# First norm summed on VectorE, columns of both streams at once, background sums put off, unread products on TensorE

## The chip, the cores and the metric

The kernel runs on one core of one Trainium2 chip. A core has five engines with queues of their own: TensorE (PE in the profile; its weight loads are shown as PEld), VectorE (DVE), ScalarE (ACT), GpSimd (POOL) and SyncE (SP), and 16 DMA engines that move data between the chip's memory and the core's own. An engine takes its instructions in order. The metric is the device time of one execution in microseconds (us); the time of a kernel is the median of its runs.

## The reference

Two layers over a stream of 256 latent tokens and a stream of 256 context tokens, with 1024 features. Each layer is an FFN, a token mixer (latent attention in layer 0, windowed attention in layer 1) and an FFN. What matters here is the first sub-layer of layer 0:

```python
cond_x = jax.nn.silu(c)
cond_c = jax.nn.silu(c_ctx)
mx = jnp.split((cond_x @ mod_w[layer] + mod_b[layer])[:, None, :], N_MOD, axis=-1)
mc = jnp.split(cond_c @ mod_w[layer] + mod_b[layer], N_MOD, axis=-1)
x = x + 0.5 * mx[2] * swiglu(modulate(rms_norm(x, norm_g[layer, 0]), mx[0], mx[1]), ffn_w_in[layer, 0], ffn_w_out[layer, 0])
xc = xc + 0.5 * mc[2] * swiglu(modulate(rms_norm(xc, norm_g[layer, 0]), mc[0], mc[1]), ffn_w_in[layer, 0], ffn_w_out[layer, 0])
...
rms_norm(x, g) = x * rsqrt(mean(x * x, axis=-1) + 1e-6) * g
modulate(h, shift, scale) = h * (1.0 + scale) + shift
swiglu(h, w_in, w_out): g, u = split(h @ w_in, 2); (silu(g) * u) @ w_out
```

Shift, scale and gate of all nine chunks come from one product of the conditioning vectors with mod_w (the adaLN). It is needed before the first normalised input exists: chunks 0 and 1 first, chunk 2 when the first FFN adds its result, the others later.

## The kernel before

The activations lie transposed: 8 tiles of 128 features (k = 0 to 7) by 512 columns, 256 latent tokens and 256 context tokens. Each float32 operand of a large product is split in a high half (rounded by ACT, L182) and a low half (the rest, by VectorE or POOL, L183), and `mm3` issues three matmuls for a pair: high by high (L210), high by low (L211), low by high (L212). Weights come as 128x1024 tiles through a ring of three raw buffers, four high and four low ones. One output tile of the FFN's first product is 8 k by 3 = 24 matmuls of 512 columns.

The order within each engine's queue is set by a scheduler when the kernel is built; `behind` holds an instruction back until another has been issued. SP issues nearly all DMAs, in order.

The start runs as follows. SP loads the constants (`load_const`, L66), the 8 tiles of x (L76), then for each k the four parts of the adaLN columns of chunks 0 and 1 (`load_column`, L120, tensor `modo`), with four first weights (`win`) between them. The norm: ACT squares each x tile (L823), TensorE sums over features by a product with ones into one bank of 128x512 (L824), so every partition holds the sum of every token; ACT takes the root (L841) and VectorE the reciprocal (L842) over 128x256 for each stream, into the strips `rstds`. For each k `mod_on_pe` multiplies the conditioning vectors by the columns (L128), ACT copies the result (L131), TensorE transposes it (L133), and VectorE adds the two halves and the bias and forms 1 + scale times the norm's gain, for one stream after the other (L138 to L140). `inputs(k)` then scales x for each stream (VectorE, L847) and makes the high (ACT, L849) and low half (VectorE, L850) of the first FFN's input.

As soon as input k exists, it is multiplied by the weights of the first four output tiles that are there by then, the lead weights (`lead_products`, `lead_weight`). Their low halves are made on POOL (L183, `wlo<-big,whi`), one at the start, the others after k = 1, 3 and 5.

Then `ffn` runs over 22 tiles f in three groups (8, 7, 7), with two weights each: gate (`og`) and up (`ou`). Between tiles `pump` issues steps of the background work: `mod_in_background` sums the adaLN of chunks 2 to 7 on VectorE, one k tile of mod_w per step, with one 128x1024 sum per stream (L149, L151), and after eight of these two small steps. Chunk 2 is needed when group 0 closes. `closing` has a step for each of the outputs d.

## Time and profile before

| | |
|---|---|
| median of 3 runs | 1734.75 us (1734.36 to 1736.54) |
| profiled execution | 1734.44 us |
| its span, first to last instruction | 1732.5 us |
| TensorE busy | 1682.6 us, 97% |
| VectorE busy | 1065.3 us, 61% |
| ScalarE busy | 666.9 us, 38% |
| GpSimd busy | 185.2 us, 11% |
| mean granted TensorE clock | 0.991 |
| HBM read and written | 240.11 and 1.05 MB |

A row of the timeline gives start and duration in us, the engine, the line of the kernel, the operation, output<-inputs with shapes and types, how many instructions the row merges (x), and in brackets how long the engine had been idle before and what ended that. "SPq" is a DMA issue of SP. A row of a waits view gives the waiting engine and line, the one waited for, the total in us, how often, and the longest. A row of the groups gives line, engine, operation, count | busy time and mean ns of one | idle time before. Granted clock 1.00 is full speed. Chains and waits are inferred, and a busy TensorE is not TensorE at its peak.

### The profile page before, as it was taken

The numbers are of one execution on the slowest core, as the hardware profiler recorded it, in microseconds if no ns is written. First come the engines' busy times: TensorE is split into PE (matmuls) and PEld (weight loads), VectorE is DVE, ScalarE is ACT, GpSimd is POOL, SyncE is SP. The second block draws the span as 40 slices with busy tenths as digits, with TensorE's granted clock in tenths as the row PEclk, the third lists the DMA queues.
The fourth block names the chain that finished last, engine by engine and source line by source line (L and its number), as shares of the span: only waits on it lengthen the run. The fifth ranks groups of instructions, "written<-read, shape, count | busy, mean of one in ns | idle before, by whom it ended". The sixth has DMA issues, their size and how long they took to land.

```text
span 1732.5 us, 24034 instructions
## 1 busy us (share of the span) xinstructions
PE 1682.6 (97%) x9512; PEld 1440.9 (83%) x9512; DVE 1065.3 (61%) x1592; ACT 666.9 (38%) x1135; POOL 185.2 (11%) x183
## 2 busy tenths in 40 slices
PE   7999999999999999999999999999999988989997
PEld 4688888888788898888888898888888888889997
DVE  4877576645667567856946374635433589755554
ACT  4322222225556352222222352222222577554443
POOL 1000000004132130000000220000000452110001
PEclk9999999999999999999999999999999999999998
DMA  8566355431212136644645254634222221145553
GB/s 331 187 199 195 129 188 189 147 125 64 86 49 72 51 98 203 198 147 156 219 126 172 93 173 160 215 121 161 94 98 92 93 85 46 53 148 182 173 191 99
DMA packets 72831, 242.71 MB, mean 140 GB/s; under 512 B 8848, under 2 KB 10640, under 8 KB 72720
## 3 DMA queue, kind: packets, MB, share of 16 engines
q1 hardware_dynamic: 72720, 241.20, 42.3%
q8 instruction: 74, 1.21, 0.3%
q14 instruction: 37, 0.30, 0.1%
HBM read 240.11 MB, written 1.05 MB: 139 GB/s over the span
## 4 chain that ended last, share of the span: by engine, by line
PE 87%; DVE 5%; issue 2%; ACT 2%; POOL 1%; DMA 1%; SPq 0%; POOLq 0%; ACTq 0%; DVEq 0%
PE bank L210 28%; PE bank L211 28%; PE bank L212 28%; DVE r2k L183 1%; DVE small L451 1%; PE bank L157 1%; DVE wlo L183 1%; DMA r2k<-in_modo 1%; PE bank L479 1%; PE bank L223 0%; POOL wlo L183 0%; PE bank L102 0%; DMA big<-in_win 0%; DVE r2k L294 0%; ACT r2k L182 0%
## 5 line engine op out<-in xcount | busy, mean ns | idle before, releaser
L210 PE MATMUL bank<-r2k,whi 128*128 128x512 f32 (+1 forms) x2610 | 915.2, 352 | 4.0 <-ACT r2k L185 2.4
L212 PE MATMUL bank<-r2k,wlo 128*128 128x512 f32 (+1 forms) x2610 | 911.8, 350 | 4.3 <-POOL wlo L183 2.2
L211 PE MATMUL bank<-r2k,whi 128*128 128x512 f32 (+1 forms) x2610 | 912.4, 350 | 3.1 <-DVE r2k L186 1.2
L182 ACT CAST whi<-wraw 128x1024 fp32r<-128x1024 f32 (+1 forms) x313 | 321.7, 1028 | 885.7 <-PE bank L211 521.8
L210 PEld LDWEIGHTS bank<-r2k,whi 128*128 128x128 f32 x2610 | 493.5, 190 | 83.1 <-ACT whi L182 9.2
L212 PEld LDWEIGHTS bank<-r2k,wlo 128*128 128x128 f32 x2610 | 494.7, 190 | 69.6 <-POOL wlo L183 3.1
L211 PEld LDWEIGHTS bank<-r2k,whi 128*128 128x128 f32 x2610 | 495.0, 190 | 68.2 <-DVE r2k L186 1.9
L183 DVE TENSOR_TENSOR wlo<-wraw,whi 128x1024 fp32r<-128x1024 f32 (+1 forms) x302 | 363.1, 1204 | 138.9 <-ACT whi L182 131.9
L151 DVE SCALAR_TENSOR_TENSOR big<-modraw,conds,big 128x1024 f32<-128x1024 f32 x196 | 242.3, 1279 | 13.1 <-DMA modraw<-in_modw 12.1
L364 DVE SCALAR_TENSOR_TENSOR x<-bank,mod,x 128x256 f32<-128x256 f32 x192 | 86.1, 479 | 180.4 <-PE bank L212 180.4
L248 POOL TENSOR_TENSOR strip<-strip 128x256 f32<-128x256 f32 x64 | 65.7, 1041 | 1116.5 <-ACT strip L242 765.5
L425 DVE TENSOR_TENSOR tmp<-bank,tmp 128x512 f32<-128x512 f32 (+1 forms) x88 | 54.9, 624 | 179.6 <-PE bank L212 177.7
L183 DVE TENSOR_TENSOR r2k<-bank,r2k 128x512 fp32r<-128x512 f32 (+2 forms) x107 | 62.1, 616 | 18.9 <-ACT r2k L182 18.5
L182 ACT CAST r2k<-bank 128x512 fp32r<-128x512 f32 (+2 forms) x107 | 52.4, 542 | 16.8 <-PE bank L212 16.0
L183 DVE TENSOR_TENSOR r2k<-tmp,r2k 128x512 fp32r<-128x512 f32 (+1 forms) x88 | 54.4, 618 | 1.5 <-ACT r2k L182 1.4
L182 ACT CAST r2k<-tmp 128x512 fp32r<-128x512 f32 (+1 forms) x88 | 49.7, 566 | 10.1 <-DVE tmp L425 9.8
L423 ACT ACTIVATE tmp<-bank 128x512 f32<-128x512 f32 (+1 forms) x88 | 47.3, 537 | 6.8 <-PE bank L212 6.7
L451 DVE TENSOR_REDUCE small<-bank 128x1 f32<-128x512 f32 (+1 forms) x64 | 37.7, 613 | 0.3 <-PE bank L652 0.2
L242 ACT ACTIVATE strip<-x 128x256 f32<-128x256 f32 x80 | 30.6, 410 | 17.8 <-DVE x L364 17.0
L186 DVE SCALAR_TENSOR_TENSOR r2k<-r2k,mod 128x256 fp32r<-128x256 f32 x45 | 28.3, 652 | 8.4 <-ACT r2k L185 7.8
L457 ACT ACTIVATE tmp<-bank,small 128x512 f32<-128x512 f32 x32 | 21.8, 687 | 18.4 <-DVE small L453 14.6
L104 DVE TENSOR_TENSOR mod<-bank,c_modb 128x4 f32<-128x4 f32 x56 | 5.2, 153 | 36.9 <-PE bank L102 36.9
(158 smaller groups left out, 1072.5 us busy)
## 6 DMA issues: line engine op xcount, KB each, us to landing
wraw<-in_win SPq DMA_DIRECT2D x172, 512.0 KB, 3.5
modraw<-in_modw SPq DMA_DIRECT2D x128, 512.0 KB, 4.2
wraw<-in_wout SPq DMA_DIRECT2D x64, 448.0 KB, 3.3
wraw<-in_wout SPq DMA_DIRECT2D x32, 512.0 KB, 3.6
r2k<-in_modo SPq DMA_DIRECT2D x32, 256.0 KB, 5.8
wraw<-in_mwo SPq DMA_DIRECT2D x8, 512.0 KB, 3.5
wraw<-in_swq SPq DMA_DIRECT2D x8, 512.0 KB, 3.5
wraw<-in_swo SPq DMA_DIRECT2D x8, 512.0 KB, 3.4
```

Source lines behind the costliest of these rows:

```text
L151: nc.vector.scalar_tensor_tensor(acc[s], raw, conds[:, kt, s:s + 1], acc[s], ALU.mult, ALU.add)
L182: nc.scalar.copy(hi, src)
L183: return engine.tensor_tensor(lo, src, hi.bitcast(F32), ALU.subtract)
L210: nc.tensor.matmul(o, lhsT=ah, rhs=bh, start=(i == 0), stop=False)
L211: nc.tensor.matmul(o, lhsT=ah, rhs=bl, start=False, stop=False)
L212: nc.tensor.matmul(o, lhsT=al, rhs=bh, start=False, stop=(i == n - 1))
L242: nc.scalar.activation(q, x, AF.Square)
L248: nc.gpsimd.tensor_tensor(self.parts[0], self.parts[0], q, ALU.add)
L364: nc.vector.scalar_tensor_tensor(xs[d][:, SL[s]], o[:, SL[s]], mod[l][:, s, c:c + 1], xs[d][:, SL[s]], ALU.mult, ALU.add)
L423: nc.scalar.activation(sg[:, :w], og[:, :w], AF.Silu)
L425: nc.vector.tensor_tensor(pr[:, :w], ou[:, :w], sg[:, :w], ALU.mult)
L451: nc.vector.tensor_reduce(top[:, j:j + 1], o[:, :w], axis=AX.X, op=ALU.max)
```

## The change

Six edits, all in the start and in the first FFN:

- The four constants that are needed first are loaded on ACT's queue, and x in four DMAs of two tiles instead of eight of one, with the array laid out for that. x is then first on SP's queue.
- `fill(n)` issues n float32 products of ones by ones, 128x128x128, into a bank that nobody reads: 40 at the start, 3 behind the transpose of column 0, and 5 behind that of column 1.
- The first norm: VectorE adds up the eight squared tiles; TensorE reduces the sum over partitions by four one-column products, so that a token stands on a partition; root and reciprocal work on 128x4; four transposes with the identity spread it over all partitions again, and ACT copies it to the strips.
- `mod_on_pe` handles both streams in each VectorE instruction: three instead of six per column. For column 1 they are held back until the input of column 0 is complete.
- The low halves of lead weights 2 to 4 are made by VectorE, the first by POOL as before.
- `ffn` of the first FFN has no background steps at tiles 0 and 1, and three instead of two at tiles 12 to 15.

TensorE's queue from the program's first instruction, before (L824 is the norm's sum, L128 and L133 the adaLN columns, L210 to L212 the products of the first lead weight):

```order
L824 MATMUL bank<-tmp,ones 128x512 x8
L128 MATMUL bank<-r2k,cond_87 32x128 x16
L133 MATMUL bank<-c_ident,tmp 128x128
L128 MATMUL bank<-r2k,cond_87 32x128 x16
L133 MATMUL bank<-c_ident,tmp 128x128
L210 MATMUL bank<-r2k,whi 128x512
L211 MATMUL bank<-r2k,whi 128x512
L212 MATMUL bank<-r2k,wlo 128x512
```

And after the change (L88 are the unread products, L843 and L849 the norm, L141 and L146 the columns, L221 to L223 the lead products):

```order
L88 MATMUL bank<-ones 128x128 x40
L843 MATMUL bank<-ones,tmp 128x1 x4
L849 MATMUL bank<-c_ident,small 128x128 x4
L141 MATMUL bank<-r2k,cond_124 32x128 x16
L146 MATMUL bank<-c_ident,tmp 128x128
L88 MATMUL bank<-ones 128x128 x3
L141 MATMUL bank<-r2k,cond_124 32x128 x16
L146 MATMUL bank<-c_ident,tmp 128x128
L88 MATMUL bank<-ones 128x128 x5
L221 MATMUL bank<-r2k,whi 128x512
L222 MATMUL bank<-r2k,whi 128x512
L223 MATMUL bank<-r2k,wlo 128x512
```

The norm's products now come behind forty unread ones and ahead of column 0, and eight more unread ones stand ahead of the first lead product.

VectorE's queue around columns 1 and 2, after the change (L153 to L155 are the column's sums, L869 and L872 scaled strip and low half, L194 the low half of the second lead weight):

```order
L153 TENSOR_TENSOR mod_127<-bank,c_modb 128x2x2
L154 TENSOR_TENSOR mod_127<-bank,mod_127 128x2x2
L155 SCALAR_TENSOR_TENSOR coefA_129<-mod_127,c_ng 128x2
L869 SCALAR_TENSOR_TENSOR strip<-x,coefA_129,strip 128x256 x2
L872 SCALAR_TENSOR_TENSOR r2k<-strip,mod_127,r2k 128x256 x2
L194 TENSOR_TENSOR wlo<-big,whi 128x1024
L153 TENSOR_TENSOR mod_127<-bank,c_modb 128x2x2
L154 TENSOR_TENSOR mod_127<-bank,mod_127 128x2x2
L155 SCALAR_TENSOR_TENSOR coefA_129<-mod_127,c_ng 128x2
```

Before, no weight's split stood in VectorE's queue between the columns; now one does behind columns 1, 3 and 5, ahead of the next column's sums.

VectorE's queue at the end of the columns and the start of the FFN's fifth weight, before:

```order
L850 SCALAR_TENSOR_TENSOR r2k<-strip,mod_90,r2k 128x256 x2
L885 TENSOR_SCALAR minus_sink<-c_sink 128x16
L149 TENSOR_SCALAR big<-modraw,conds 128x1024 x2
L151 SCALAR_TENSOR_TENSOR big<-modraw,conds,big 128x1024 x2
L183 TENSOR_TENSOR wlo<-wraw,whi 128x1024
L425 TENSOR_TENSOR tmp<-bank,tmp 128x512
```

And after:

```order
L872 SCALAR_TENSOR_TENSOR r2k<-strip,mod_127,r2k 128x256 x2
L907 TENSOR_SCALAR minus_sink<-c_sink 128x16
L194 TENSOR_TENSOR wlo<-wraw,whi 128x1024
L437 TENSOR_TENSOR tmp<-bank,tmp 128x512 x2
L194 TENSOR_TENSOR r2k<-tmp,r2k 128x512
L194 TENSOR_TENSOR wlo<-wraw,whi 128x1024
L194 TENSOR_TENSOR r2k<-tmp,r2k 128x512
L164 TENSOR_SCALAR big<-modraw,conds 128x1024 x2
```

The first four background sums, which stood ahead of the fifth weight's low half, now come behind the low halves of the fifth and the sixth.

The diff, cut to its core:

```diff
-    def load_const(name, shape, dtype=F32):
+    def load_const(name, shape, dtype=F32, queue=nc.sync):
...
-        nc.sync.dma_start(s, t[name])
+        queue.dma_start(s, t[name])
...
+    cond_raw = load_const("cond", (P, KT, 2), queue=nc.scalar)
+    ident = load_const("ident", (P, P), queue=nc.scalar)
+    modb = load_const("modb", (P, 2, 72), queue=nc.scalar)
+    ng = load_const("ng", (P, 2, 3, KT), queue=nc.scalar)
...
-    for d in range(KT):
-        nc.sync.dma_start(xs[d], t["xT"][d])
+    for d in range(0, KT, 2):
+        nc.sync.dma_start(x_all[:, d:d + 2], t["xT"][:, d:d + 2])
...
+    def fill(n, after=None):
+        b = bank()
+        with behind(after):
+            for _ in range(n):
+                nc.tensor.matmul(b[:, :P], lhsT=ones, rhs=ones, start=True, stop=True)
...
+    fill(40)
...
-    def mod_on_pe(k, raws):
+    def mod_on_pe(k, raws, n=0, after=None):
...
-        nc.tensor.transpose(psB, sA, ident)
+        turned = nc.tensor.transpose(psB, sA, ident)
+        if n:
+            fill(n, turned)
...
-        for s in range(2):
-            v = mod[0][:, s, :2 * KT].rearrange("p (c k) -> p c k", c=2)[:, :, k]
-            bias = modb[:, 0, :2 * KT].rearrange("p (c k) -> p c k", c=2)[:, :, k]
-            nc.vector.tensor_tensor(v, vB[:, :, 0, s], bias, ALU.add)
-            nc.vector.tensor_tensor(v, vB[:, :, 1, s], v, ALU.add)
-            nc.vector.scalar_tensor_tensor(coefA[0][:, s, 0, k:k + 1], v[:, 1:2], 1.0, ng[:, 0, 0, k:k + 1], ALU.add, ALU.mult)
+        v = mod[0][:, :, :2 * KT].rearrange("p s (c k) -> p c s k", c=2)[:, :, :, k]
+        bias = modb[:, 0, :2 * KT].rearrange("p (c k) -> p c k", c=2)[:, :, k:k + 1].to_broadcast([P, 2, 2])
+        with behind(after):
+            nc.vector.tensor_tensor(v, vB[:, :, 0, 0:2], bias, ALU.add)
+        nc.vector.tensor_tensor(v, vB[:, :, 1, 0:2], v, ALU.add)
+        nc.vector.scalar_tensor_tensor(coefA[0][:, :, 0, k], v[:, 1], 1.0, ng[:, 0, 0, k:k + 1].to_broadcast([P, 2]), ALU.add, ALU.mult)
...
-    def ffn(sl, nxt, per_tile=0):
+    def ffn(sl, nxt, per_tile=0, late=0):
...
-                pump(per_tile // 2, done)
+                n = 0 if f < late else per_tile + (6 * late <= f < 8 * late)
+                pump(n // 2, done)
                 og = next(outs)
-                pump(per_tile - per_tile // 2, done)
+                pump(n - n // 2, done)
...
-    total = bank()
+    squares = None
     for d in range(KT):
         q = tmp()
         nc.scalar.activation(q, xs[d], AF.Square)
-        nc.tensor.matmul(total, lhsT=ones, rhs=q, start=(d == 0), stop=(d == KT - 1))
+        if squares is None:
+            squares = q
+        else:
+            nc.vector.tensor_tensor(squares, squares, q, ALU.add)
     load_table(AF.Sqrt, q)
+    total = bank()
+    for j in range(4):
+        nc.tensor.matmul(total[:, j:j + 1], lhsT=squares[:, j * P:(j + 1) * P], rhs=ones[:, 0:1], start=True, stop=True)
+    root = small()
+    nc.scalar.activation(root, total[:, 0:4], AF.Sqrt, scale=1.0 / D, bias=eps)
+    nc.vector.reciprocal(root, root)
+    wide = bank()
+    for j in range(4):
+        nc.tensor.transpose(wide[:, j * P:(j + 1) * P], root[:, j:j + 1].to_broadcast([P, P]), ident)
+    rstds = [strip() for _ in range(2)]
+    for r, cols in zip(rstds, SL):
+        nc.scalar.copy(r, wide[:, cols])
...
-            wt = weight_split(wraws[len(sl.lead)], nc.gpsimd)
+            wt = weight_split(wraws[len(sl.lead)], nc.vector if sl.lead else nc.gpsimd)
...
-    rstds = [strip() for _ in range(2)]
-    for s, r in enumerate(rstds):
-        nc.scalar.activation(r, total[:, SL[s]], AF.Sqrt, scale=1.0 / D, bias=eps)
-        nc.vector.reciprocal(r, r)
...
-    mod_on_pe(0, raws[0])
+    mod_on_pe(0, raws[0], 3)
...
-            mod_on_pe(k, raws[k])
+            mod_on_pe(k, raws[k], 5 if k == 1 else 0, sl.end if k == 1 else None)
...
-    ffn(sl, nxt, 2)
+    ffn(sl, nxt, 2, 2)
...
-    put("xT", np.concatenate([x[0].T, ctx[0].T], axis=1).reshape(KT, P, TT))
+    put("xT", np.concatenate([x[0].T, ctx[0].T], axis=1).reshape(KT, P, TT).transpose(1, 0, 2))
```

More of the change, by code (lines that the diff above doesn't have):

```diff
@@ L81, in hybrid_backbone_kernel, with behind @@
     nc.vector.memset(eps, EPS)
+    def fill(n, after=None):
[3 more added lines that the diff above has]
+                nc.tensor.matmul(b[:, :P], lhsT=ones, rhs=ones, start=True, stop=True)
+    def behind(ins):
+        return tc.issue_after(ins.ins) if ins else nullcontext()
+    fill(40)
     conds = const.tile([P, KT, 2], F32, name="conds")
@@ L161, in mod_in_background @@
         yield
-    def behind(ins):
-        return tc.issue_after(ins.ins) if ins else nullcontext()
     background = []
```

4 lines of the change are left out of this document (removed).

## The prediction

> **What bounds the kernel now.** I read the profile's page first, then TensorE's waits, then the timeline of the first 70 us. The page says that TensorE is nearly always busy:
>
> ```profile
> span 1732.5 us, 24034 instructions
> ...
> PE 1682.6 (97%) x9512; PEld 1440.9 (83%) x9512; DVE 1065.3 (61%) x1592; ACT 666.9 (38%) x1135; POOL 185.2 (11%) x183
> ```
>
> So a change that adds and removes no real matmul can only win back idle or half-speed TensorE time. The diff touches the time before the first FFN product and the first FFN itself. The waits of TensorE there (first three rows: from 0 to 100 us; last row, the only one of its view: from 66 to 380 us) are:
>
> ```profile
> PE bank L824 <- ACT tmp L823: 6.1, 1, 6.1
> PE bank L212 <- POOL wlo L183: 2.2, 2, 1.1
> PE bank L212 <- DVE wlo L183: 2.0, 1, 2.0
> ...
> PE bank L102 <- ACT tmp L97: 0.3, 1, 0.3
> ```
>
> Everything that can be won lies ahead of about 65 us; behind it the first FFN waits 0.3 us in 314. A second loss is the clock. Columns of these stretches: busy time of PE, PEld, DVE, ACT, POOL, then granted clock, DMA share, GB/s:
>
> ```profile
> 20.00:23.00 3.00, 0.80 (x2) 0.48 (x3) 2.96 (x13) 2.56 (x5) 0.00 (x0) 1.00 1.06 407
> 23.00:27.00 4.00, 4.00 (x39) 2.84 (x39) 0.70 (x5) 0.61 (x2) 2.35 (x1) 0.57 1.04 408
> 57.00:60.00 3.00, 1.30 (x6) 0.75 (x4) 3.00 (x3) 2.97 (x6) 0.00 (x0) 1.00 0.49 178
> 60.00:65.00 5.00, 4.72 (x14) 3.71 (x15) 4.87 (x7) 3.24 (x5) 0.00 (x0) 0.66 0.85 279
> 66.00:380.00 314.00, 313.67 (x1411) 253.75 (x1410) 213.03 (x254) 84.19 (x106) 0.00 (x0) 1.00 0.53 172
> ```
>
> Twice about 3 us with TensorE busy for 0.80 and 1.30 us are followed by a spell below full clock: 4 x 0.43 = 1.7 us of work lost at 23 us and 5 x 0.34 = 1.7 us at 60 us.
>
> **The norm and the first loads (term A).** What runs before the first useful product:
>
> ```profile
> 0.74 0.38 SPq L66 DMA_DIRECT2D c_cond<-in_cond  x1
> ...
> 2.58 0.43 SPq L76 DMA_DIRECT2D x<-in_xT  x1
> ...
> 6.14 8.91 PE L824 MATMUL bank<-tmp,ones 128*128 128x512 f32 x16 [6.14 <-ACT tmp L823]
> ...
> 11.09 1.29 ACT L823 ACTIVATE tmp<-x 128x512 f32<-128x512 f32 x2 [0.40 <-DMA x<-in_xT]
> ...
> 15.60 3.36 DVE L842 RECIPROCAL strip<-strip 128x256 f32<-128x256 f32 x2 [11.81 <-ACT strip L841]
> ...
> 19.41 0.48 DVE L847 SCALAR_TENSOR_TENSOR strip<-x,coefA,strip 128x256 f32<-128x256 f32 x1
> ...
> 23.37 1.94 PE L128 MATMUL bank<-r2k,cond 128*32 128x128 f32 x32
> ...
> 31.07 1.08 PE L128 MATMUL bank<-r2k,cond 128*32 128x128 f32 x32
> ```
>
> Before, four constants are issued on SP ahead of x. After, x is SP's first work: its first issue moves from 2.58 to 0.74, 1.84 us earlier, and the modo columns behind it move as much. The constants now stand in ACT's queue ahead of its table load; by SP's pitch four issues end at about 2.6. This is hidden: the row of 11.09 shows ACT waiting for x, still at the last pair. The last squares end at 11.09 + 1.29 - 1.84 = 10.5, and the seventh VectorE add (about 0.68, as L425 below) at 11.2.
>
> TensorE is kept by the 40 fills till then. Their price is not in the trace; the nearest rows are 128x128 float32 transposes in a row, the weight loads of one-column products, and the old norm's loads:
>
> ```profile
> 497.40 1.03 PE L479 MATMUL bank<-c_ident,tmp 128*128 128x128 f32 x8
> ...
> 406.57 0.78 PE L223 MATMUL bank<-ones,strip 128*128 128x1 f32 x6
> ...
> 8.01 0.34 PEld L824 LDWEIGHTS bank<-tmp,ones 128*128 128x128 f32 x1 [0.52 <-issue]
> 8.86 0.34 PEld L824 LDWEIGHTS bank<-tmp,ones 128*128 128x128 f32 x1 [0.52 <-ACT tmp L823]
> ...
> 10.60 0.19 PEld L824 LDWEIGHTS bank<-tmp,ones 128*128 128x128 f32 x1 [0.24 <-issue]
> 11.03 0.19 PEld L824 LDWEIGHTS bank<-tmp,ones 128*128 128x128 f32 x1 [0.24 <-issue]
> ...
> 407.39 0.26 ACT L225 ACTIVATE small<-bank,eps 128x2 f32<-128x2 f32 x1 [0.92 <-PE bank L223]
> ...
> 407.69 0.17 DVE L226 RECIPROCAL small<-small 128x2 f32<-128x2 f32 x1 [1.73 <-ACT small L225]
> ...
> 408.43 0.37 ACT L231 COPY strip<-bank 128x256 f32<-128x256 f32 x1 [0.78 <-PE bank L229]
> ```
>
> Eight transposes in 1.03 us, the last lasting 0.27, are 0.109 apart. A float32 matmul is two instructions (8 matmuls of L824 are x16), so a fill takes 0.22. The old norm's loads stand 0.85 apart at first and 0.43 from about 10 us on, 3.6 us after its start: TensorE starts at half speed. Forty fills from 1.05 us: 3.6 us for the first 8, then 32 x 0.22, so to 11.7. If a whole 0.27 were paid per instruction, a fill would be 0.54; I take 0.22, the pitch of the same shape, and keep 0.54 for a rival.
>
> The new chain from 11.7: eight one-column instructions 1.1 (x6 took 0.78), root 0.26, reciprocal 0.17, four transposes 0.6, two copies 0.74, hand-overs 0.2: the strips stand at 14.8 instead of 18.96. But the gain shrinks at once. Column 0's products follow the transposes (13.8, one group 1.1), and ACT casts the first weight (1.06 by the cast further below) ahead of that column's copy: its sums start at about 16.4. There POOL's split of the first weight runs from 15.8 to 18.2, and these rows show what VectorE then does:
>
> ```profile
> 33.46 2.37 POOL L183 TENSOR_TENSOR wlo<-big,whi 128x1024 fp32r<-128x1024 f32 x1 [7.69 <-ACT whi L182]
> ...
> 34.52 1.32 DVE L140 SCALAR_TENSOR_TENSOR coefA<-mod,c_ng 128x1 f32<-128x1 f32 x1
> ...
> 35.89 0.50 PE L212 MATMUL bank<-r2k,wlo 128*128 128x512 f32 x1 [1.10 <-POOL wlo L183]
> ...
> 40.67 0.16 DVE L140 SCALAR_TENSOR_TENSOR coefA<-mod,c_ng 128x1 f32<-128x1 f32 x1
> ```
>
> A scalar_tensor_tensor of 0.16 takes 1.32 and ends when POOL ends, at 35.83. So the first scaled strip comes at 18.2 against 19.41. Its operands need one more strip or activation and two remainders after it, all 256 wide like the 0.48 of L847, say 0.5 + 0.55 + 2 x 0.55 with hand-overs: TensorE's second product at 20.4, column 2 at 20.9 against 23.37. Loads are no limit: the modo columns land 1.84 us earlier too.
>
> From there VectorE takes some back: the second weight's split (1.2) now stands in its queue ahead of column 2's sums. With split, cast and products in a row I get 26.0 for column 3 and 29.0 for column 4 against 31.07, though the 1.7 us of the first half-speed spell are gone: the 3 and 5 fills fill TensorE's gaps there. **A = 2.1**; bounds: 1.2 (the first strip) and 4.2 (the strips of the norm). The columns of both streams at once save three instructions of about 0.15 of six on VectorE, per column; ACT's two activations per column set the pace, so 0 (at most 8 x 0.15 = 1.2, inside A's bounds).
>
> **Lead weights on VectorE (B).** The two waits for POOL's low halves, 1.1 each, go, and with them the locked VectorE. The new split costs VectorE 1.2 for 2.37 on POOL. It queues behind both activations of columns 3 and 5; TensorE may wait 0.2 to 0.5 for it each time, but loses no lock. **B = 2.2**, bounds 1.2 and 2.8.
>
> **Background sums later (C, D).** The stall at the FFN's start:
>
> ```profile
> 56.11 1.06 ACT L182 CAST whi<-wraw 128x1024 fp32r<-128x1024 f32 x1 [1.33 <-PE bank L211]
> ...
> 56.62 2.47 DVE L151 SCALAR_TENSOR_TENSOR big<-modraw,conds,big 128x1024 f32<-128x1024 f32 x2
> ...
> 59.01 1.22 DVE L183 TENSOR_TENSOR wlo<-wraw,whi 128x1024 fp32r<-128x1024 f32 x1
> ...
> 60.28 0.50 PE L212 MATMUL bank<-r2k,wlo 128*128 128x512 f32 x1 [1.98 <-DVE wlo L183]
> ```
>
> The high half is ready at 57.17, but VectorE is in a background sum. Without it the low half is done at 57.2 + 1.22 = 58.4 instead of 60.2. **C = 1.8** of the 1.98 (bounds 1.5 and 1.98). With the idle stretch gone, the half-speed spell behind it should go: **D = 1.7** (bounds 0 and 1.7).
>
> Put off, these sums come at tiles 12 to 15, three steps each:
>
> ```profile
> L183 DVE TENSOR_TENSOR wlo<-wraw,whi 128x1024 fp32r<-128x1024 f32 x237 | 292.7, 1237 | 118.6 <-ACT whi L182 112.0 <-PE bank L479 0.6
> ...
> L151 DVE SCALAR_TENSOR_TENSOR big<-modraw,conds,big 128x1024 f32<-128x1024 f32 x196 | 242.3, 1279 | 13.1 <-DMA modraw<-in_modw 12.1 <-DVE big L151 0.4
> ...
> L425 DVE TENSOR_TENSOR tmp<-bank,tmp 128x512 f32<-128x512 f32 x66 | 45.5, 690 | 163.9 <-PE bank L212 162.6 <-ACT tmp L423 1.4
> ```
>
> A tile there is 2 x 1.24 + 2 x 0.69 (the product and its split, of one size) + 6 x 1.28 = 11.5 us of VectorE against 48 matmuls x 0.22 = 10.7 of TensorE (314 us over 1411 instructions, above). That lag of 0.8 per tile, over four tiles, is covered by the three raw and four split buffers, and two steps in ten are only small. Cost 0, at most 4 x 0.8 = 3.2.
>
> **Sum.** 2.1 + 2.2 + 1.8 + 1.7 = 7.8. The profiled execution took 1734.44, 0.3 below the median of 1734.75, so 1734.44 - 7.8 = **1726.6**.
>
> **Rivals.** First, the half-speed spell at 60 us has another cause and stays: D = 0, 1728.3. For it: the waits of 1.1 us for POOL brought no spell. Against: both spells follow 3 us that were at most 43% busy. The Trainium skill, "TensorE: Matmul & The Clock Gate", section "HAM oscillation — how this bites in real kernels", speaks for this rival: it asks for "no PE-idle gaps >~3.4µs", which a stall of 1.98 keeps. The traces as they stand contradict it, with a spell behind each stretch of shorter gaps.
>
> Second, the front gains nothing (A = 0): VectorE's chain (columns, then a split) eats the earlier norm, 1728.7. For it: between columns 1 and 2 cast, split and sums now stand in one row, and TensorE may idle enough there for a spell of its own.
>
> Third, on the slower side: the fills outlast the data. At 0.54 per fill the 40 end 40 x 0.32 = 12.8 us later, and the norm, everything behind it too: 1739.4. The gain is gone from 0.22 + 7.8/40 = 0.42 per fill on, and it is 0.2% slower from 0.51 on. Against it stands the pitch of 0.109.
>
> **How the numbers follow.** Two tenths of a per cent (3.5 us) is about what a measurement of this kernel can tell from no change. Forecast 0.52; clock rival 0.18; front rival 0.12; a larger gain, with A near 4.2 (1724.5), 0.08; both first rivals or waits in tiles 12 to 15 together (1730.4 to 1733.6), 0.05; fills too long, 0.05. Faster holds the first four, 0.90, less 0.01 for spells that move elsewhere; same 0.06; slower 0.05. The range reaches from A's upper bound with one spell of 1.7 fewer elsewhere, 1722.8, to the front rival with C's lower bound (0.3) and half of the lag's bound (1.6), 1730.6.
>
> **What would show it.** In the changed profile: fills ending near 11.7 and the strips near 14.8; the first scaled strip near 18.2, at POOL's end; no TensorE wait for POOL ahead of 60 us; the first FFN weight's low half following its cast; full clock from 12 to 70 us; nothing moved behind 400 us but by the shift. I am wrong if the fills end after 14, if VectorE's splits become TensorE's waits, or if a spell stands where none was.

## Result and profile after

The changed kernel takes 1725.66 us (median of 4 runs, 1723.45 to 1726.01); the kernel before, run beside it, 1735.07 (1734.36 to 1736.54). The ratio is 0.9942, 95% interval 0.9927 to 0.9957: faster by 9.4 us by the medians. The forecast was 1726.6, range 1722.8 to 1730.6. The profiled execution took 1725.39 against 1734.44: 9.05 less, where the prediction's sum was 7.8.

The top of the page of the changed kernel:

```profile
span 1723.5 us, 24196 instructions
...
PE 1685.7 (98%) x9604; PEld 1449.6 (84%) x9604; DVE 1067.4 (62%) x1577; ACT 665.0 (39%) x1136; POOL 177.7 (10%) x180
```

TensorE is busy 3.1 us longer, for the unread products count as busy, and yet the span is 9.0 shorter. TensorE's largest waits from 0 to 100 us:

```profile
PE bank L88 <- DVE ones L79: 1.1, 1, 1.1
PE bank L146 <- ACT tmp L144: 0.8, 2, 0.4
PE bank L849 <- DVE small L846: 0.6, 1, 0.6
```

The 2.2 for POOL and the 2.0 for VectorE's low half are gone. Windows of the changed kernel (busy time of PE, PEld, DVE, ACT, POOL, then granted clock, DMA share, GB/s):

```profile
14.00:17.40 3.40, 3.01 (x40) 2.49 (x39) 0.68 (x3) 1.86 (x4) 1.56 (x1) 0.56 1.00 381
...
20.00:23.00 3.00, 2.90 (x43) 1.98 (x41) 2.71 (x9) 1.46 (x4) 0.00 (x0) 1.00 1.05 399
23.00:27.00 4.00, 3.82 (x43) 2.33 (x42) 3.26 (x9) 1.50 (x4) 0.00 (x0) 1.00 1.04 405
...
60.00:65.00 5.00, 5.00 (x23) 4.14 (x23) 5.00 (x6) 1.05 (x1) 0.00 (x0) 1.00 0.77 239
66.00:380.00 314.00, 314.00 (x1413) 254.21 (x1412) 214.70 (x258) 84.66 (x108) 3.70 (x4) 1.00 0.53 174
```

Both half-speed spells of before (clock 0.57 at 23 to 27 us, 0.66 at 60 to 65) are gone; a new one runs from 14.4 to 17.8 us (0.56 in the first row). The last row says that the sums put off to tiles 12 to 15 cost TensorE nothing: 314.00 busy of 314. The steps of the start, from the timeline (start, duration, engine, line):

```profile
1.05 10.66 PE L88 MATMUL bank<-ones 128*128 128x128 f32 x80 [1.05 <-DVE ones L79]
11.87 1.05 PE L843 MATMUL bank<-ones,tmp 128*128 128x1 f32 x8 [0.15 <-DVE tmp L839]
...
14.17 0.65 ACT L852 COPY strip<-bank 128x256 f32<-128x256 f32 x2 [0.95 <-PE bank L849]
...
17.05 1.17 DVE L155 SCALAR_TENSOR_TENSOR coefA<-mod,c_ng 128x2 f32<-128x2 f32 x1
18.32 0.88 DVE L869 SCALAR_TENSOR_TENSOR strip<-x,coefA,strip 128x256 f32<-128x256 f32 x2
...
52.06 1.23 DVE L194 TENSOR_TENSOR wlo<-wraw,whi 128x1024 fp32r<-128x1024 f32 x1 [1.63 <-ACT whi L193]
53.34 0.50 PE L223 MATMUL bank<-r2k,wlo 128*128 128x512 f32 x1
```

The fills end at 11.71, the norm's strips stand at 14.82, the first scaled strip starts at 18.32, and the fifth weight's low half follows its cast at once: its first product comes at 53.34, against 60.28 before. That is 6.94 earlier; behind the spell at 60 us, which is gone too, the shift grows to the 9.05, for instance at the first long run of one-column products behind the first FFN (before, then after):

```profile
406.57 0.78 PE L223 MATMUL bank<-ones,strip 128*128 128x1 f32 x6
```

```profile
397.52 0.78 PE L234 MATMUL bank<-ones,strip 128*128 128x1 f32 x6
```

This place is the ruler of what follows, since it holds all that the change does and nothing of what differs between executions later. What differs between executions ahead of it stays in: the kernel before and experiment 12 are the same up to column 7 and stand 1.27 apart there. "Columns" are the groups of one adaLN column's products on TensorE. One row is one kernel; columns and place are of its profiled execution, the median and the ratio are of 4 to 11 runs, against runs of the kernel before beside them (medians 1735.56, 1735.53 and 1734.52 for experiments 1 to 4, 5 to 8 and 9 to 12).

| kernel | us | ratio, 95% | column 4 | column 7 | place |
|---|---|---|---|---|---|
| before | 1735.07 | 1 | 31.07 | 50.68 | 406.57 |
| changed | 1725.66 | 0.9942, 0.9927 to 0.9957 | 28.67 | 45.90 | 397.52 |
| 1 sums not late | 1731.02 | 0.9972, 0.9962 to 0.9983 | 28.69 | 45.95 | 404.30 |
| 2 and stall filled | 1731.58 | 0.9976, 0.9966 to 0.9986 | 29.02 | 46.28 | 404.96 |
| 3 lead weights on POOL | 1729.41 | 0.9962, 0.9949 to 0.9976 | 31.82 | 51.31 | 402.85 |
| 4 old norm, no 40 fills | 1726.50 | 0.9942, 0.9930 to 0.9955 | 28.55 | 45.81 | 397.91 |
| 5 old columns | 1726.21 | 0.9951, 0.9938 to 0.9963 | 29.04 | 46.49 | 398.97 |
| 6 column 1 not held | 1725.37 | 0.9940, 0.9927 to 0.9954 | 28.52 | 45.78 | 397.45 |
| 7 constants ahead of x | 1726.61 | 0.9947, 0.9934 to 0.9959 | 31.17 | 48.38 | 400.07 |
| 8 all lead weights on VectorE | 1724.77 | 0.9937, 0.9925 to 0.9950 | 28.81 | 46.05 | 397.52 |
| 9 before + leads + late sums | 1729.02 | 0.9966, 0.9953 to 0.9978 | 32.01 | 49.44 | 402.17 |
| 10 before + loads | 1734.94 | 1.0002, 0.9993 to 1.0011 | 31.41 | 51.03 | 406.94 |
| 11 before + loads, leads, late sums | 1727.85 | 0.9961, 0.9948 to 0.9975 | 30.70 | 48.10 | 400.25 |
| 12 before + late sums | 1732.60 | 0.9986, 0.9977 to 0.9995 | 32.31 | 51.95 | 404.58 |

### The profile page after: what moved, and what is told of

It is laid out like the page before. It is cut to its first block, busy times and chain, and to the rows that moved or that the text cites. A ratio compares the mean times of both kernels' runs of the same rounds, so it can differ in the third digit from the quotient of the medians.

```text
span 1723.5 us, 24196 instructions
## 1 busy us (share of the span) xinstructions
PE 1685.7 (98%) x9604; PEld 1449.6 (84%) x9604; DVE 1067.4 (62%) x1577; ACT 665.0 (39%) x1136; POOL 177.7 (10%) x180
## 3 DMA queue, kind: packets, MB, share of 16 engines
HBM read 240.11 MB, written 1.05 MB: 140 GB/s over the span
## 4 chain that ended last, share of the span: by engine, by line
PE 88%; DVE 5%; ACT 2%; issue 2%; DMA 1%; POOL 1%; SPq 0%; ACTq 0%; POOLq 0%; DVEq 0%
PE bank L221 28%; PE bank L222 28%; PE bank L223 28%; DVE r2k L194 1%; DVE small L463 1%; PE bank L172 1%; DVE wlo L194 1%; PE bank L491 1%; PE bank L234 0%; DMA big<-in_win 0%; DMA c_ng<-in_ng 0%; PE bank L115 0%; DVE r2k L305 0%; ACT r2k L193 0%; DVE r2k L528 0%
## 5 line engine op out<-in xcount | busy, mean ns | idle before, releaser
L221 PE MATMUL bank<-r2k,whi 128*128 128x512 f32 (+1 forms) x2610 | 914.3, 352 | 2.7 <-ACT r2k L196 2.4
L223 PE MATMUL bank<-r2k,wlo 128*128 128x512 f32 (+1 forms) x2610 | 911.2, 349 | 0.2
L221 PEld LDWEIGHTS bank<-r2k,whi 128*128 128x128 f32 x2610 | 493.0, 190 | 81.0 <-ACT whi L193 10.1
L223 PEld LDWEIGHTS bank<-r2k,wlo 128*128 128x128 f32 x2610 | 494.4, 189 | 65.5 <-DVE wlo L194 1.4
L194 DVE TENSOR_TENSOR wlo<-wraw,whi 128x1024 fp32r<-128x1024 f32 (+1 forms) x302 | 363.0, 1204 | 137.0 <-ACT whi L193 130.2
L194 DVE TENSOR_TENSOR r2k<-bank,r2k 128x512 fp32r<-128x512 f32 (+2 forms) x107 | 62.2, 617 | 18.9 <-ACT r2k L193 18.5
L194 DVE TENSOR_TENSOR r2k<-tmp,r2k 128x512 fp32r<-128x512 f32 (+1 forms) x88 | 54.4, 618 | 1.4 <-ACT r2k L193 1.4
```

The costliest lines, as they stand in the source:

```text
L194: return engine.tensor_tensor(lo, src, hi.bitcast(F32), ALU.subtract)
L221: nc.tensor.matmul(o, lhsT=ah, rhs=bh, start=(i == 0), stop=False)
L223: nc.tensor.matmul(o, lhsT=al, rhs=bh, start=False, stop=(i == n - 1))
```

## Experiments

**1. The late sums undone** (terms C and D).

```
-    ffn(sl, nxt, 2, 2)
+    ffn(sl, nxt, 2)
```

> The changed kernel with its late background sums undone: the FFN pumps two steps a tile from its first tile on, as before; norm, fills and lead weights stay changed. By the prediction's terms C and D come back: VectorE is in a background sum when the fifth weight's high half is cast, TensorE waits about 2.0 us for the low half, and a half-speed spell that costs about 1.7 us follows near 55 to 60 us. So 3.5 to 4.1 us above the changed kernel (about 1729.3 against its 1725.66). If the spell had another cause (the clock rival), the stall of 2.0 comes back without a spell: 2.0 above, 1727.7. If the three steps a tile at tiles 12 to 15 had cost something (up to 3.2), the kernel would lose less than that by this undoing: 0.5 to 1.

Measured: 6.8 later at the place, 5.2 in the ratio's median (0.9972 - 0.9942 of 1735). Its largest wait from 0 to 100 us, and windows of 3.4 us, laid so that one begins with the spell:

```profile
PE bank L223 <- DVE wlo L194: 4.6, 2, 2.5
```

```profile
53.50:56.90 3.40, 0.93 (x4) 0.80 (x5) 3.40 (x5) 3.40 (x7) 0.00 (x0) 1.00 0.67 245
56.90:60.30 3.40, 3.40 (x10) 2.61 (x9) 3.40 (x4) 0.68 (x1) 0.00 (x0) 0.50 0.65 192
67.10:70.50 3.40, 2.14 (x10) 1.44 (x8) 3.40 (x5) 1.08 (x2) 0.00 (x0) 1.00 0.47 154
70.50:73.90 3.40, 2.51 (x11) 2.10 (x12) 3.40 (x4) 0.35 (x1) 0.00 (x0) 1.00 0.76 210
```

There are two stalls, not one: 2.50 before 55.97 and 2.15 before 71.39. VectorE is busy for all of each row (3.40), so with column 7 4.7 earlier than before TensorE runs further ahead of VectorE, and the part is worth 6.8 here where the prediction saw 3.5. Only the first stall is followed by a spell (clock 0.50). The three steps a tile at tiles 12 to 15 cost nothing.

**2. The same with the stall filled** by unread products.

```
+                    if self.l == 0 and self.sub == 0 and i == len(self.lead):
+                        fill(10, self.led)
                     mm3(o[:M, :w], ...
... (self.led is the last lead product; the late sums are undone as in 1)
```

> As the kernel with the late sums undone, but with ten unread 128x128 products (0.22 each, 2.2 us) in TensorE's row where it waits for the fifth weight's low half; the wait itself stays, for VectorE's background sum is still ahead of the split. So C stays undone and only TensorE's idleness is taken away. If the half-speed spell behind the stall comes from the idle TensorE (the prediction's D), no slice near 55 to 62 us is below full clock, and the time is 1.7 less than that of the kernel with the sums undone: 2.0 to 2.4 above the changed kernel, about 1727.9. If the spell has another cause (the clock rival: the rule of the Trainium skill that a stall of 2 us is too short to bring one), it stands in this kernel as in that without the products, and the two times agree: 3.7 above, about 1729.4.

```profile
70.61 0.50 PE L223 MATMUL bank<-r2k,wlo 128*128 128x512 f32 x1 [1.92 <-DVE wlo L194]
```

```profile
53.50:56.90 3.40, 3.15 (x24) 2.63 (x23) 3.40 (x5) 3.39 (x8) 0.00 (x0) 1.00 0.68 235
56.90:60.30 3.40, 3.40 (x17) 2.80 (x16) 3.40 (x3) 1.02 (x2) 0.00 (x0) 1.00 0.64 206
```

```profile
67.90:71.30 3.40, 1.48 (x7) 0.94 (x6) 3.40 (x5) 1.67 (x2) 0.00 (x0) 0.99 0.72 242
71.30:74.70 3.40, 3.40 (x10) 2.66 (x9) 3.40 (x4) 0.00 (x0) 0.00 (x0) 0.51 0.64 205
```

No stretch behind the filled stall is below full clock: the spell there does come from the idle TensorE, and the clock rival falls. The time is no better all the same, against both expectations: the second stall (1.92, shorter than the 2.15 of experiment 1) now has a spell behind it. So the length of the wait alone does not decide it. In the kernel before (rows below), here and in experiment 1, what goes ahead of a spell of 3.4 us is a stretch of 3.4 us with TensorE busy for 0.93 to 1.48; the second stall of experiment 1 lies across two such stretches (busy 2.14 and 2.51) and brings none.

```profile
57.60:61.00 3.40, 1.42 (x7) 0.87 (x6) 3.40 (x5) 3.37 (x5) 0.00 (x0) 0.99 0.69 210
61.00:64.40 3.40, 3.40 (x10) 2.62 (x9) 3.27 (x4) 2.24 (x4) 0.00 (x0) 0.50 0.84 298
```

Every spell that the clock shows in the first 100 us of these profiles lasts 3.41 us or twice that (read in windows of 0.1 us), and the two of the kernel before begin 37.55 apart (23.41 and 60.96), 11 times 3.41.

The Trainium skill, "TensorE: Matmul & The Clock Gate", section "What's actually happening", has an activity window of about 3.4 us that runs freely; these rows agree. Its rule of gaps over 3.4 us, which the prediction cited, does not hold here: stalls of 1.92, 1.98 and 2.50 brought spells.

**3. Lead weights on POOL again** (term B).

```
-            wt = weight_split(wraws[len(sl.lead)], nc.vector if sl.lead else nc.gpsimd)
+            wt = weight_split(wraws[len(sl.lead)], nc.gpsimd)
```

> The changed kernel with the low halves of all lead weights on POOL again, as before. By term B: TensorE's two waits for POOL's low halves of about 1.1 come back, near 31 and 42 us, with the short VectorE instruction that ends when POOL ends; the last column starts 2.2 to 2.4 later than in the changed kernel (48.1 to 48.3 against 45.90), and the time is 2.2 to 2.4 above it, about 1728. If the waits only take the place of others (rival), the last column starts within 1 us of 45.9 and the time is less than 1 above. If the new waits also bring a half-speed spell, 1.7 more: 4.

Measured: column 7 5.4 later, the place 5.3; 3.5 by the ratios' medians, with intervals that overlap a little. TensorE's waits, then one window (PE busy, clock, DMA share, GB/s):

```profile
PE bank L223 <- POOL wlo L194: 3.7, 3, 1.5
```

```profile
27.00:30.00 3.00, 3.00 (x36) 0.50 1.07 420
```

Three waits for POOL, not two: the second weight's low half, which TensorE did not wait for before, is late too, since the front is earlier. It brings a spell (about 1.7). 3.7 + 1.7 is the 5.4: the expectation's third case and one wait more.

**4. The old norm, without the 40 products ahead of it.**

```
-    fill(40)
...
-            nc.vector.tensor_tensor(squares, squares, q, ALU.add)
+        nc.tensor.matmul(total, lhsT=ones, rhs=q, start=(d == 0), stop=(d == KT - 1))
... (root and reciprocal of 256 tokens a strip, as before, behind the first lead weight)
```

> The changed kernel with the old norm: the eight squares summed by TensorE's eight 128x512 float32 products, the root and the reciprocal over 256 tokens a strip, and without the 40 unread products ahead of it (the 3 and 5 behind columns 0 and 1 stay, as do the joined loads of x, the columns of both streams at once, the lead weights and the late sums). By term A (measured: column 4 starts 2.4 earlier than before): strips near 18.9 again, column 4 near 30.8 to 31.1 against 28.67, and the time 2.0 to 2.4 above the changed kernel, about 1727.9. If the norm was not what the front waited for (the front rival: the chain of columns and splits is the limit), column 4 starts within 0.7 of 28.67, and the time is less than 0.7 above.

```profile
14.68 3.37 DVE L853 RECIPROCAL strip<-strip 128x256 f32<-128x256 f32 x2 [8.25 <-ACT strip L852]
...
18.50 0.88 DVE L858 SCALAR_TENSOR_TENSOR strip<-x,coefA,strip 128x256 f32<-128x256 f32 x2
...
20.50 0.50 PE L221 MATMUL bank<-r2k,whi 128*128 128x512 f32 x1
```

The strips stand at 18.05 instead of 14.82, and the first scaled strip still starts at 18.50 against 18.32, the second product even earlier (20.50 against 20.81). Column 4, the place and the time are those of the changed kernel. The part that gives the change its name is worth nothing here, and the expectation of 2.0 to 2.4 fell.

**5. The old columns**: one stream after the other, and column 1's sums not held.

```
-        with behind(after):
-            nc.vector.tensor_tensor(v, vB[:, :, 0, 0:2], bias, ALU.add)
...
+        for s in range(2):
+            nc.vector.tensor_tensor(v, vB[:, :, 0, s], bias, ALU.add)
... (the loop of before)
```

> The changed kernel with the old code of the adaLN column sums: one stream after the other, three short VectorE instructions each, and column 1's sums not held behind column 0's second remainder. Norm, unread products, loads, lead weights and late sums stay changed. The old norm in place of the new one cost nothing (column 4 at 28.55 against 28.67), so the gain at column 4 has another source. Theory: the order on VectorE. Before, the sums and scaled strips of columns 0 and 1 ran ahead of column 0's remainders (first strip 19.41, first remainder 21.78: 2.37 apart; in the changed kernel 18.32 and 19.68). Then here the first remainder comes 1.0 to 1.3 later than in the changed kernel, TensorE's second product near 21.8 to 22, column 4 near 29.9 to 31, and, where TensorE's idle time ahead of 23 us brings a half-speed spell, 1.7 more. Time 1.2 to 3 above the changed kernel (1726.7 to 1728.5). Rival (the prediction's: columns cost 0, the norm and the loads carry it): column 4 within 0.4 of 28.67, time within 0.4 of 1725.5.

```profile
22.24 0.49 PE L222 MATMUL bank<-r2k,whi 128*128 128x512 f32 x1 [1.19 <-DVE r2k L872]
```

The second product is 1.4 later, as the theory said, but column 4 only 0.37 and column 7 0.6; the place is 1.45 later. No spell follows (clock 1.00 from 20 us on): the unread products behind the columns are still there. Time 1.6 more by the ratios, intervals overlapping.

**6. Only the hold of column 1's sums undone.**

```
-            mod_on_pe(k, raws[k], 5 if k == 1 else 0, sl.end if k == 1 else None)
+            mod_on_pe(k, raws[k], 5 if k == 1 else 0)
```

> The changed kernel in which only the hold is undone: column 1's sums no longer wait for column 0's second remainder; the columns of both streams stay in one instruction. VectorE then runs column 1's three sums and two scaled strips (1.4 us) ahead of column 0's remainders. If the order is what counts, nearly all of what the old column code costs shows here too: TensorE's second product 1.2 to 1.4 later, column 4 1.0 to 1.4 later. If the six short instructions in place of three are what counts, column 4 stays within 0.4 of 28.67.

TensorE waits 1.1 for the remainder here as well, but column 3 has caught up (25.80 against 25.88) and column 4 and the place are 0.1 earlier. The hold is worth nothing: VectorE's split of the second weight then comes 1.05 earlier (22.41 against 23.46). My theory that the order on VectorE carries the gain fell.

**7. The constants ahead of x on SP again.**

```
-    cond_raw = load_const("cond", (P, KT, 2), queue=nc.scalar)
+    cond_raw = load_const("cond", (P, KT, 2))
... (ident, modb and ng likewise)
```

> The changed kernel with the four constants issued on SP ahead of x, as before, instead of on ACT. SP's first issue of x moves from 0.74 to about 2.6, all that stands behind it on SP by as much, but the constants land at 1.7 to 2.3 instead of 3.9 to 7.0, so that SP's later issues don't wait for them. If x's start is on the path, the strips of the norm come 1.0 to 1.8 later and column 4 0.7 to 1.8 later; time 1 to 2 above the changed kernel. If the modo columns and weights are what the front waits for and those are held by the rate of the DMA engines (1.05 busy from 5 to 35 us), column 4 within 0.4 of 28.67 and the time the same.

```profile
14.20 1.05 PE L843 MATMUL bank<-ones,tmp 128*128 128x1 f32 x8 [1.80 <-DVE tmp L839]
```

The norm comes 2.3 later, the columns 2.3 to 2.8, the place 2.5, more than the 0.7 to 1.8 expected. So x, through the norm, is on the path of the changed kernel; whether the loads behind x on SP are on it too, this run does not separate. (Of the 2.5 the runs' ratios show 0.9, with overlapping intervals.)

**8. All lead weights on VectorE**, tried as a better version.

```
-            wt = weight_split(wraws[len(sl.lead)], nc.vector if sl.lead else nc.gpsimd)
+            wt = weight_split(wraws[len(sl.lead)], nc.vector)
```

> The changed kernel with the first lead weight's low half on VectorE too, so that POOL does nothing in the first 60 us. In the changed kernel VectorE's coefficient instruction (0.16 elsewhere) lasts 1.17 there and ends with POOL's split at 18.19. Without it the split takes VectorE from 15.8 to 17.0, the sums follow, and the first scaled strip starts near 17.6 instead of 18.32: 0.7 earlier up to column 4, time 0.4 to 0.7 less than the changed kernel (about 1724.9). Rival: the second product waits for the weight's high half, the columns or the loads (DMA engines 1.05 busy): column 4 within 0.3 of 28.67 and no change.

```profile
13.02 0.95 PE L843 MATMUL bank<-ones,tmp 128*128 128x1 f32 x8
...
16.85 1.23 DVE L194 TENSOR_TENSOR wlo<-big,whi 128x1024 fp32r<-128x1024 f32 x1 [2.37 <-ACT whi L193]
...
18.39 0.16 DVE L155 SCALAR_TENSOR_TENSOR coefA<-mod,c_ng 128x2 f32<-128x2 f32 x1
```

The coefficient instruction is back at 0.16 without POOL, so the 1.17 was POOL's doing. (The Trainium skill, "SBUF — State Buffer", section "SBUF: two separate sides", has POOL and a VectorE instruction with two SBUF inputs share one lock for a whole instruction; the rows agree.) But in this execution the fills ended at 13.19 instead of 11.71 and held the norm (13.02 against 11.87, no wait ahead of it). Counted from ACT's cast of the weight (15.76 against 14.71), the first scaled strip comes 0.78 earlier than in the changed kernel, as expected; the late fills took it back, and the place is the same to 0.01. Nothing gained that the runs can tell: 0.9937 against 0.9942.

**9. Before, with the lead weights and the late sums alone** (all of term A left out). The edits are those of the diff's hunks on `lead_weight`, `ffn` and its call; nothing else changes.

```
+            wt = weight_split(wraws[len(sl.lead)], nc.vector if sl.lead else nc.gpsimd)
...
+    ffn(sl, nxt, 2, 2)
```

> The kernel before with two parts of the change alone: the low halves of lead weights 2 to 4 on VectorE and the late background sums. Loads, norm, columns and unread products are as before; so the difference to the changed kernel is the whole of term A. Measured by the one-column products behind the first FFN, which start at 406.57 before and at 397.52 in the changed kernel: if A is worth what the prediction took (2.1) or what column 4 showed (2.4), they start at 399.6 to 400.0 here, time about 1727.7. If undoing the loads alone already costs 2.55 (as with the constants ahead of x), at 400.1 and no later. If A is worth nothing once the lead weights are on VectorE (front rival): below 398.5. If the idle time ahead of 23 us brings its half-speed spell back as well: up to 401.8.

Measured: the place at 402.17, so A is worth 4.65 in the presence of B, C and D; 4.2 by the ratios (0.9966 - 0.9942). That is nearest to the last case: a half-speed spell stands here (first row below), from 20.94 to 27.77, twice as long as the one of before.

**10 and 11. Before with the loads alone; and with loads, lead weights and late sums** (no new norm, no unread product, old columns).

```
+    cond_raw = load_const("cond", (P, KT, 2), queue=nc.scalar)
... (ident, modb, ng likewise)
+    for d in range(0, KT, 2):
+        nc.sync.dma_start(x_all[:, d:d + 2], t["xT"][:, d:d + 2])
... (in 11 also the edits of 9)
```

> The kernel before with the loads alone changed: constants on ACT's queue, x first on SP in four loads of two blocks. Norm, columns, lead weights and background sums as before, no unread products. If the place of x on SP is what term A came from (constants ahead of x cost the changed kernel 2.5 at every column), columns 2 to 4 start 1.8 to 2.5 earlier than before (column 4 at 28.6 to 29.3 against 31.07) and the time is 1.8 to 2.5 less than before. If the earlier x only moves the old norm's start (6.14 to 5.44 with the same loads in the kernel with the old norm) and POOL's splits, the two columns in one row on VectorE and the half-speed spell at 23 us stay what they are, column 4 comes 0.7 earlier, time 0.7 less.

> The kernel before with the loads, the lead weights on VectorE and the late sums of the change, and without the rest of it: old norm, old columns of one stream after the other, no unread product anywhere. If norm, unread products and columns bring nothing together, the one-column products behind the first FFN start within 0.7 of 397.52 and the time is that of the changed kernel (ratio to before 0.994). The old columns alone cost 1.45 at that place (398.97) in the changed kernel: then 399.0. If the unread products behind columns 0 and 1 are what keeps the clock up there, a slice near 20 to 27 us stands below full clock and it is 1.7 more: 400.7.

Windows of 23 to 27 us: experiment 9, then 10, then 11 (PE busy, clock, DMA share, GB/s):

```profile
23.00:27.00 4.00, 3.83 (x36) 0.50 1.05 408
```

```profile
23.00:27.00 4.00, 4.00 (x38) 0.50 1.04 402
```

```profile
23.00:27.00 4.00, 4.00 (x40) 0.61 1.04 403
```

The loads alone gain nothing (1.0002; column 4 0.34 later), less than either case: the old norm's products begin 0.7 earlier (5.4 for 6.1) but column 0's only 0.13 (14.85 for 14.98), POOL's waits stay at 2.2 and the spell stays (20.45 to 27.27). With the lead weights on VectorE the same loads show 1.3 at column 7 and 1.9 at the place (9 to 11), but 0.9 by the ratios, whose intervals overlap widely; and 9 has the long spell, 11 a short one (22.74 to 26.16). Experiment 12 will show that this much can differ between two executions of one front, so a gain from the loads is not shown. The place of 11, 400.25, is nearest to the last case of its expectation. Between 11 and 4, which have the same old norm and loads, stand only the joined columns with their hold and the 3 and 5 unread products: 2.3 at either place. The spell makes 4 x 0.39 = 1.6 of it, and it is gone in 4 and in 5, both of which keep the unread products. No run takes these eight products out alone, so that they end the spell is likely and not shown.

**12. Before, with the late sums alone.**

```
-    ffn(sl, nxt, 2)
+    ffn(sl, nxt, 2, 2)
```

> The kernel before with the late background sums alone. By the prediction's C and D: the stall of 1.98 at 58.3 goes but for a rest of 0.3, the half-speed spell behind it goes, and the one-column products behind the first FFN start 3.5 to 3.7 earlier, at 402.9 to 403.1; time 1731. The undoing of the same part in the changed kernel cost 6.8 at that place, for there VectorE's sums made two stalls (2.5 and 2.15) and one spell. If the part were worth the same here: at 399.8, time 1728.5.

Measured: the place 1.99 earlier, the time 1.9 less by the medians. But this execution had reached column 7 1.27 later than the profile of before (51.95 against 50.68), though nothing ahead of it is changed: column 0 began at 15.62 against 14.98, and the spell is twice as long, 6.83 us (21.39 to 28.21) instead of 3.41 (23.41 to 26.82). Two windows of experiment 12 (PE busy, clock, DMA share, GB/s); in the profile of before the clock is 1.00 in both:

```profile
20.00:23.00 3.00, 0.80 (x1) 0.73 1.06 409
...
27.00:30.00 3.00, 3.00 (x26) 0.80 1.04 401
```

From column 7 on it gains 3.26, near the 3.5 to 3.7 expected.

## Why the prediction was right in sum, and wrong in one step

**C and D held.** From column 7 to the place: 355.89 before, 351.62 after, so 4.27 gained, of which the rest of the stall is 2.06 (from the start of the product ahead to that of the fifth weight's first low-half product: 2.37, now 0.31) and the spell 1.7. Of the remaining 0.5, 0.3 is the wait of L102, which is gone. That the spell hangs on the stall is shown by experiment 2.

**B held in its size.** Column 4 to column 7 takes 2.38 less (17.23 against 19.61); the prediction took 2.2. Experiments 12 and 9, which differ by the lead weights alone and both have the long spell, give 2.5 at column 7.

**A's size was bounded, its cause was wrong.** At column 4 the kernel is 2.4 earlier, against 2.1 predicted, and the dated steps held to 0.5 us: fills, strips, first scaled strip, columns 2 (21.37, predicted 20.9), 3 (25.88, 26.0) and 4 (28.67, 29.0). That 2.4 is so near to 2.1 is in part luck: against the other profile with the front of before (12), which has the long spell, column 4 is 3.6 earlier. Measured by leaving all of A out (9), which has the long spell as well, it is worth 3.3 at column 4, 3.5 at column 7 and 4.65 at the place, where the upper bound was 4.2; by the ratios it is 4.2. And its parts, taken in the order 9, 11, 4, changed, at column 7: loads 1.3, about what two profiles of one front differ by; joined columns and the unread products behind columns 0 and 1, 2.3; new norm and its 40 products, -0.1. The step that failed is the one that let the norm's strips (14.8 for 18.96) carry the gain. In its place the runs show the joined columns, which the prediction put at 0, together with the 3 and 5 unread products, which it did name, with the end of the first spell, and set against VectorE's split. The strips were early for nobody: column 0's own sums are not there until 16.65, and POOL's split of the first weight holds the next instruction till 18.19. That split is late because ACT's cast of the weight stands behind the norm's copies. In experiment 4 it stands ahead of the roots, and cast and split run 2.1 earlier; there VectorE's reciprocals hold the sums, until 18.05. The rows of the changed kernel, then of 4:

```profile
14.71 1.06 ACT L193 CAST whi<-big 128x1024 fp32r<-128x1024 f32 x1
...
15.84 2.35 POOL L194 TENSOR_TENSOR wlo<-big,whi 128x1024 fp32r<-128x1024 f32 x1 [15.40 <-ACT whi L193]
```

```profile
12.63 1.04 ACT L192 CAST whi<-big 128x1024 fp32r<-128x1024 f32 x1 [1.12 <-DMA big<-in_win]
...
13.75 2.36 POOL L193 TENSOR_TENSOR wlo<-big,whi 128x1024 fp32r<-128x1024 f32 x1 [13.31 <-ACT whi L192]
```

So two paths of nearly equal length lead to the first scaled strip (18.32, and 18.50 in 4): one through the new norm, the cast and POOL's split, one through the old norm's reciprocals. The new norm shortens the second and lengthens the first. A cast that stands ahead of the new norm's copies was not tried.

The chain that the profile draws for the changed kernel seems to say otherwise, that loads pace the start up to 23.45 (start, duration, what; the last row is a cast from its timeline):

```profile
11.45 7.06 DMA big<-in_win
18.53 4.92 DMA r2k<-in_modo
23.46 1.24 DVE wlo L194
```

```profile
22.40 1.03 ACT L193 CAST whi<-big 128x1024 fp32r<-128x1024 f32 x1
```

But the split at 23.46 reads no column: its operands are the weight, landed at 18.51, and the cast, which ends at 23.43. In experiments 1, 4, 7 and 8 the same split starts 0.03 to 0.04 behind its cast and is put down to it. The landing at 23.45 only fell beside it. So nothing here refutes "Loads are no limit" for the columns and weights; that x itself is on the path, experiment 7 shows.

**"The modo columns land 1.84 us earlier too"** held for SP's first modo issue (4.64 for 6.38) and for little behind it: the second weight lands at 18.51 for 19.29, 0.8 earlier, as SP's later issues wait for the constants that moved to ACT's queue (last section). **"Full clock from 12 to 70 us"** was wrong from 14.4 to 17.8, on which little hung. The copy of column 0 waits for ACT's cast until 15.77 anyway. But the unread products and column 1 behind it are slower, so that column 1's copy stands in ACT's way at 18.97 (18.37 in experiment 1, which has no spell there): ACT's first activation starts 0.81 behind the first scaled strip, there 0.51.

**The rivals.** The clock rival fell by experiment 2. The front rival (A = 0) fell by experiment 9, though what it said of the norm came true (4). The rival of fills that outlast the data happened in small: the pitch of 0.104 warm is as predicted, but in five of the eight profiled executions with the new norm (the changed kernel and experiments 1 to 3 and 5 to 8) its first product follows the fills without a wait, at 12.27 to 13.02 instead of 11.87. Column 4 then stands at 28.5 to 29.0 in those of the five with the lead weights on VectorE. Part of the delay comes back because no spell follows there (clock 1.00 from 14 to 20 us).

**The parts do not add up in the profiles.** Taken away one at a time, late sums, lead weights, constants' place, columns and norm cost 6.8 + 5.3 + 2.5 + 1.5 + 0.4 = 16.5 at the place, and all together 9.05. By the ratios of the runs it is 5.2 + 3.5 + 0.9 + 1.6 + 0.0 = 11.2 against 10.1, which their intervals cannot tell from a plain sum. What the traces of 1 and 3 do show: a part, once undone in a kernel that is otherwise early, opens a gap that the others' delays had covered (the second stall of 1, the third wait of 3), and a gap can bring a spell of 1.7.

## What to carry to other kernels

Before an operand that comes earlier is counted as a gain, ask what else its first user waits for, and what the change puts in the way of that: here the strips came 3 us sooner, the first weight's cast 2.1 later, and nothing was gained. A chain's links are inferred, so compare a link with what the instruction reads before building on it. Price a part in both contexts, taken away from the new kernel and added to the old; here they differ by a factor of two (late sums: 6.8 and 3.3 by the profiles, 5.2 and 2.4 by the ratios). And ask what two executions of the same code differ by: here a spell of 3.41 or 6.83 us, with 1.27 between them at column 7, as much as some parts seemed to be worth. A gap of 2 us in TensorE's work cost up to 1.7 more behind it; a few unread products in the gap took that away, but in experiment 2 the next gap brought the spell back.

## What was not expected of the hardware

Small loads that share the engines with large ones are slow to land. Issues of the first 40 us, of the changed kernel and then of the kernel before (queue, count, KB, median us from issue to landing):

```profile
c_ng<-in_ng ACTq DMA_DIRECT2D x1, 24.0 KB, 7.0
c_cond<-in_cond ACTq DMA_DIRECT2D x1, 8.0 KB, 3.9
```

```profile
c_ng<-in_ng SPq DMA_DIRECT2D x1, 24.0 KB, 1.8
c_cond<-in_cond SPq DMA_DIRECT2D x1, 8.0 KB, 1.7
```

In the changed kernel SP's own waits (0 to 40 us) then show them in the middle of its loads:

```profile
SPq L133 <- DMA c_cond<-in_cond: 2.0, 1, 2.0
...
SPq L202 <- DMA c_ng<-in_ng: 0.9, 1, 0.9
```

With the constants on SP again (7) the two land after 2.0 and 1.6. So moving the constants off SP's queue gave x its place but not SP its freedom. Whether constants that are issued later, or joined into one load, would take these waits away was not tried.

The spell at 14.39 to 17.81 of the changed kernel follows a stretch (10.97 to 14.38) in which TensorE counts as busy for 2.69 of 3.41, more than ahead of any other spell (0.89 to 1.84; only experiment 5, with the same start, has 2.55). Some 1.05 of that are products with one column. If those do not count as work for the clock, 1.64 remain, which lies among the others. But in experiment 1 a stretch that lies on the raster of its own spell (12.50 to 15.91; its end is 12 times 3.41 ahead of the spell's start at 56.87) has 2.39 with 0.72 of such products, so 1.67, and no spell follows. The cause stays open.
